# The output projection in a new order of tiles, with the operands of the MLP made beside it

## The chip, the cores and the metric

The kernel runs on one core of one Trainium2 chip. The metric is the device time of one execution in microseconds. A core has TensorE (PE in the rows; PEld is its weight load), VectorE (DVE), ScalarE (ACT), GpSimd (POOL) and SyncE (SP), which issues most of the DMAs; DMAs are also issued from ACT. Each engine, and each queue of DMA issues, works through its instructions in order.

## The reference

One pre-norm decoder layer on 2048 tokens of width 1024: a token mixer (gated DeltaNet heads and dilated sliding-window attention heads), then a gated MLP with a causal depthwise convolution, then a final RMSNorm. The part around the change:

```python
x = x + jnp.concatenate([y_a, y_b], axis=-1) @ w_out[l]        # output projection
h = rmsnorm(x, ln2[l])
gate = causal_dwconv(h @ w_gate[l], ffn_conv[l])
x = x + (jax.nn.silu(gate) * (h @ w_up[l])) @ w_down[l]
```

## The kernel before

Every product of float32 numbers is made of three products of split numbers: an operand is cast to a high part on ACT and the rest is taken as a low part on DVE (`split`, L67 and L68), and `mm3` (L73 to L75) multiplies high by high, high by low and low by high.

The tokens are 16 tiles of 128. The output projection (`Mlp.out_proj`, L1025) takes one tile at a time: it loads the mixer's results for these tokens (`yg`, L1046, and `ys`, L1049, both in runs of 512 bytes), splits them, runs 48 matmuls of 512 columns, loads the tile of `x` (L1069), adds (L1072), and stores the sum as `x1` (L1073). `norm2` (L952) then works on the tile before: square and sum on ACT, two small steps on GpSimd (L902, L903), scaling on DVE (L958, in place, so it waits until `x1` is stored), eight transposes on TensorE (L962) that stand behind the next tile's matmuls, two copies on ACT (L963) and a store to `hT` in memory (L965). The first three tiles run seven of their eight row blocks ahead (`HEAD`).

The MLP (`gate_up`, L1083) works in two halves of 1024 tokens. A half is a 2 x 2 arrangement of blocks: two blocks of 512 tokens (b = 0 is the half's first four tiles, b = 1 its second four) by two halves of the width (kh). It is multiplied by a scheme of seven products, so there are seven operands s = 0 to 6, each a high and a low tile `hc[s]`. Operands 0 and 3 are parts of block 0 alone, 1 and 4 are differences of both blocks, 2 and 6 are built on those. A pass p goes through the seven steps for two blocks of 128 hidden columns; there are eleven passes for each half. Each step has 24 matmuls and needs two weight operands, made two steps ahead (`prep`): for s = 1, 2, 4 and 5 from sums on GpSimd (L1119 to L1129). The results leave the banks `g` and `sc`, `pv`, `tp` by copies on ACT (L1204) or additions on DVE (L1202).

Operands of the first half are made by `form` (L967), 512 columns at a time, from `hT`. For the second half four operands (1, 2, 4, 6: `EARLY`) are made ahead by `foresee(j)` (L994), which takes tile j of both blocks: loads of 256 KB (L1002), one to three subtractions on GpSimd (L1010), the split on GpSimd too, and two stores of 256 KB to `hf` (L1015). `recall` loads them when the second half begins; the other three are made by `form(1, s)`. `foresee`'s results take their buffers from the same three as `xt` and, later, `cv`; the loads of `form` and `foresee` share four buffers `sm`.

The order before: tiles 0 to 7, then 8, 12, 9, 13, 10, 14, 11, 15. From the eleventh place on (i >= 10) three steps of `form(0, 0..3)` follow each tile, from the thirteenth two steps of `foresee`. Eight of its 16 steps are left for gate_up, one in each of the passes p = 1 to 8. The last tile's `norm2` (`late`) comes in gate_up's first steps, with both transposes in bank `pv`; `form(0, 4..6)` in its first three.

Of the kernel before, what the change touches and what calls it, by code (L numbers as in the profile page):

```python
# [9 lines left out]
F32 = mybir.dt.float32  # L10
F32R = mybir.dt.float32r
BF16 = mybir.dt.bfloat16
AF = mybir.ActivationFunctionType
ALU = mybir.AluOpType
# [917 lines left out]
class Mlp:  # L932
# [19 lines left out]
    def norm2(self, xt, t, tag=None):  # L952
# [6 lines left out]
        for j in range(2):  # L959
            tp = n.bank(4, tag)  # L960
            for k in range(4):
                nc.tensor.transpose(tp[:, k, :], xt[:, (4 * j + k) * P:(4 * j + k + 1) * P], n.ident)  # L962
            nc.scalar.copy(xt[:, 512 * j:512 * j + 512].rearrange("p (k t) -> p k t", k=4), tp)  # L963
# [30 lines left out]
    def foresee(self, j):  # L994
# [10 lines left out]
        for s, first, rest in ((1, (1, 0), ((0, 0),)), (4, (1, 1), ((1, 0),)), (2, (0, 0), ((1, 1), (1, 0))),  # L1005
# [10 lines left out]
            yield  # L1016

    def recall(self, s):
        n = self.n
# [5 lines left out]
    def out_proj(self):  # L1025
        n, a = self.n, self.n.a
        nc, tc, v = n.nc, n.tc, n.nc.vector
        with ExitStack() as eo:
# [28 lines left out]

            first = (x for s in range(4) for x in self.form(0, s))
            for t in range(HEAD):
                out_proj(t, range(7))  # L1060
            early = self.early = (x for j in range(4) for x in self.foresee(j))
            for i, t in enumerate((*range(8), 8, 12, 9, 13, 10, 14, 11, 15)):
                out_proj(t, range(7, 8) if t < HEAD else range(8))
                if t >= HEAD:
                    for j in list(xts)[:2]:
# [7 lines left out]
                nc.sync.dma_start(n.x1[t], xt)  # L1073
                if i >= 10:
                    for _ in range(3):
                        next(first, None)
                if i >= 12:
                    next(early)
                    next(early)
            assert next(first, 1)  # L1080
            self.late = lambda: [self.norm2(xts[j], j, "pv") for j in list(xts)]

    def gate_up(self):  # L1083
# [7 lines left out]
        spare = dict(zip(("sa", "sb", "r01"), three))  # L1091
        steps = [(half, p, s) for half in range(2) for p in range(NP) for s in range(7)]
        raws, sums, made = {}, {}, {}
# [85 lines left out]
        for i, (half, p, s) in enumerate(steps):  # L1179
# [17 lines left out]
            for m in range(2):  # L1197
# [5 lines left out]
                else:  # L1203
                    nc.scalar.copy(dst, ps)  # L1204
            if half == 0:
                if p == 0 and s < 3:
                    for _ in self.form(0, s + 4):
                        pass
                if p == NP - 1:
                    if s in EARLY:  # L1210
                        self.recall(s)
                    else:
                        for _ in self.form(1, s):
                            pass
                elif p and s == 4:
                    next(self.early, None)
            if i == 1:
                self.late()
            if s == 5:
# [235 lines left out]
```

## Time and profile before

| | us |
|---|---|
| runs shown | 2839.38, 2845.15, 2848.18 |
| their median | 2845.15 |
| the profiled execution | 2836.76 |
| its span, first to last instruction | 2835.0 |

The rows of the section below come from that one profiled execution; times in them count from the start of its span. A row of the timeline has the start, the duration, the engine, the line, the operation and, in brackets, how long the engine had been idle before it and what ended that. In a row of groups, the numbers behind the bar are busy time, mean nanoseconds of one, and idle time before them.

### The profile page before, as it was taken

The page shows a single profiled execution, that of the slowest core. Times are in us where ns is not written, and L with a number is a line of the kernel's source. Part 1 is how long each engine was busy: PE and PEld are TensorE (multiplying, and loading weights), DVE is VectorE, ACT ScalarE, POOL GpSimd, SP SyncE. Part 2 cuts the span into 40 slices and gives each one's busy share as a digit, 9 for nine tenths or more (in the row PEclk, how much of TensorE's full clock was granted, in tenths as well). Part 3 has the DMA queues.
Part 4 walks back from the last instruction along what each step waited for, and adds up shares of the span by engine and source line. Part 5 has one row for each costly group of instructions (what it writes and reads, how often), then busy time and mean ns, then how long its engine had stood idle before and what let it go on. Part 6 is the DMA issues. An engine that isn't in the chain of part 4 may idle for free. (4 is left out here: it accounts for less than half of the span.)

```text
span 2835.0 us, 41316 instructions
## 1 busy us (share of the span) xinstructions
PE 2716.6 (96%) x14974; PEld 2278.4 (80%) x14974; DVE 1682.6 (59%) x2758; ACT 1111.2 (39%) x2333; POOL 1149.3 (41%) x1363
## 2 busy tenths in 40 slices
PE   8999999899999999989968999999999998999999
PEld 8998777777798998877856777777888887788887
DVE  4205544823655655644337878878877787545464
ACT  5313545252056666563224333324333333322243
POOL 4300223132244444411165777766656664312231
PEclk9999999999899999999989999999999999999999
DMA  5222343377676656347684444446333333865553
GB/s 184 81 57 96 114 133 125 104 218 209 177 197 177 181 167 171 96 125 225 199 258 134 123 138 122 127 130 237 104 104 93 112 104 128 317 232 174 184 196 136
DMA packets 398490, 438.71 MB, mean 155 GB/s; under 512 B 84247, under 2 KB 289351, under 8 KB 396871
## 3 DMA queue, kind: packets, MB, share of 16 engines
q1 hardware_dynamic: 350672, 406.76, 46.2%
q10 hardware_dynamic: 45390, 20.90, 2.8%
q0 software_dynamic: 2224, 8.42, 1.0%
q8 instruction: 118, 1.93, 0.3%
q14 instruction: 86, 0.70, 0.1%
HBM read 295.79 MB, written 140.18 MB: 154 GB/s over the span
## 5 line engine op out<-in xcount | busy, mean ns | idle before, releaser
L68 DVE TENSOR_TENSOR wl<-wr,wh 128x512 fp32r<-128x512 f32 x220 | 304.7, 1417 | 69.8 <-ACT wh L67 68.7
L67 ACT CAST wh<-wr 128x512 fp32r<-128x512 f32 x220 | 136.2, 624 | 241.2 <-POOL wr L1119 119.8
L1165 POOL TENSOR_TENSOR sm<-cv 128x512 f32<-128x512 f32 x110 | 183.7, 1701 | 38.7 <-issue 26.7
L1249 POOL TENSOR_TENSOR w<-w,w 128x512 f32<-128x512 f32 x55 | 91.7, 1688 | 228.7 <-DMA w<-in_w_down_dram 223.3
L651 DVE CUSTOM_DVE_ANT_0 s<-sc,bias 128x256 f32<-128x256 f32 (+1 forms) x384 | 121.4, 362 | 104.8 <-PE sc L643 85.1
L67 ACT CAST ah<-ar 128x1408 fp32r<-128x1408 f32 x56 | 77.1, 1378 | 251.8 <-PE tp L74 70.1
L741 PE MATMUL pv<-pt,sv 128*65 128x128 f32 x1200 | 159.9, 276 | 6.3 <-ACT pt L723 5.9
L713 ACT ACTIVATE s<-s,nm 128x256 f32<-128x256 f32 (+1 forms) x384 | 151.8, 460 | 35.6 <-POOL rb L788 25.7
L73 PE MATMUL g<-hch,wh 128*128 128x512 f32 x352 | 143.2, 407 | 23.5 <-ACT g L1204 13.1
L75 PE MATMUL g<-hch,wl 128*128 128x512 f32 x352 | 142.5, 405 | 6.4 <-DVE wl L68 6.3
L741 PEld LDWEIGHTS pv<-pt,sv 128*65 128x65 f32 x1200 | 135.4, 139 | 11.0 <-ACT pt L723 10.2
L74 PE MATMUL g<-hcl,wh 128*128 128x512 f32 x352 | 142.0, 403 | 0.0
L73 PE MATMUL sc<-hch,wh 128*128 128x512 f32 x352 | 139.5, 396 | 1.8 <-ACT u L1204 1.1
L75 PE MATMUL sc<-hch,wl 128*128 128x512 f32 x352 | 139.1, 395 | 0.4 <-DVE wl L68 0.4
L74 PE MATMUL sc<-hcl,wh 128*128 128x512 f32 x352 | 139.2, 396 | 0.0
L74 PE MATMUL tp<-hcl,wh 128*128 128x512 f32 x352 | 139.0, 395 | 0.0
L73 PE MATMUL tp<-hch,wh 128*128 128x512 f32 x352 | 139.0, 395 | 0.0
L75 PE MATMUL tp<-hch,wl 128*128 128x512 f32 x352 | 139.0, 395 | 0.0
L723 ACT COPY pt<-tp 128x512 f32<-128x512 f32 (+1 forms) x152 | 87.3, 577 | 94.0 <-PE tp L720 57.3
L1145 DVE SCALAR_TENSOR_TENSOR cv<-g,fcw,cv 128x1024 f32<-128x1024 f32 x88 | 123.1, 1399 | 1.5
L580 POOL CAST qc<-q 128x256 fp32r<-128x256 f32 x128 | 79.9, 640 | 106.4 <-PE sc L643 102.8
L331 POOL TENSOR_SCALAR ss<-ss 128x8 f32<-128x8 f32 x16 | 3.3, 204 | 289.0 <-ACT junk L330 289.0
(379 smaller groups left out, 8284.9 us busy)
## 6 DMA issues: line engine op xcount, KB each, us to landing
ar<-act SPq DMA_DIRECT2D x56, 704.0 KB, 4.1
w<-in_w_down_dram SPq DMA_DIRECT2D x132, 256.0 KB, 5.1
act<-sm SPq DMA_DIRECT2D x110, 256.0 KB, 2.4
sm<-hT SPq DMA_DIRECT2D x92, 256.0 KB, 4.6
r<-in_w_gate_dram SPq DMA_DIRECT2D x66, 256.0 KB, 3.1
r<-in_w_up_dram SPq DMA_DIRECT2D x66, 256.0 KB, 4.2
xt<-in_x_dram SPq DMA_DIRECT2D x32, 512.0 KB, 4.5
zn<-zn SPq DMA_DIRECT2D x32, 512.0 KB, 5.4
```

The lines of the kernel that those rows point to most:

```text
L67: (first or nc.scalar.copy)(hi, src)
L68: (e or nc.vector).tensor_tensor(lo, src, hi.bitcast(F32), op=ALU.subtract)
L73: nc.tensor.matmul(ps, ah, bh, start=start, stop=False, skip_group_check=more)
L74: nc.tensor.matmul(ps, ah, bl, start=False, stop=False, skip_group_check=more)
L75: nc.tensor.matmul(ps, al, bh, start=False, stop=stop, skip_group_check=more)
L651: n.mark = v.tensor_tensor_reduce(out=s[:, r], in0=ps[:, r], in1=self.bias[d][:, bo:bo + r.stop - r.start], scale=1.0, scalar=-3e38, op0=A ...
L713: nc.scalar.activation(s, s, AF.Exp, bias=nm[:, col:col + 1])
L723: nc.scalar.copy(pts[g][:, 0:o], tp[:, 0:o])
L741: nc.tensor.matmul(dst, self.vcols(h, d, u, back), pt[:, j * P:(j + 1) * P], start=(back == int(prev)), stop=(back == 0))
L1145: v.scalar_tensor_tensor(cv, g[:, j:j + 1024], self.cw[:, x, j:j + 1], cv, op0=ALU.mult, op1=ALU.add)
L1165: gp.tensor_tensor(src, x(*op_[0]), x(*op_[2]), op=ALU.add if op_[1] > 0 else ALU.subtract)
L1249: gp.tensor_tensor(wsum[i, k], wsum[i, k], t, op=ALU.add if op[1] > 0 else ALU.subtract)
```

## The change

The projection takes the second half's tokens first, and in pairs: tile j of block 0, tile j of block 1. All 16 steps of `foresee` follow the tiles of places 4 to 11, two each. For the first half, operands 0 to 3 are made by a new function, `piece(j, s)`, 128 tokens at a time, from the fifth to last place on: two after each of the last four tiles, six after the loop, and the two that need the last tile, (3, 1) and (3, 2), after gate_up's first step, behind that tile's `norm2`, whose transposes now go to the banks `g` and `sc`. The first pass of gate_up takes its steps in the order 0, 3, 1, 2, 4, 5, 6.

```diff
-            tp = n.bank(4, tag)
+            tp = n.bank(4, tag and tag[j])
...
+    def piece(self, j, s):
+        n = self.n
+        nc, v, gp = n.nc, n.nc.vector, n.nc.gpsimd
+        c = slice(j * P, j * P + P)
+        k4 = lambda x: x.rearrange("p (k t) -> p k t", k=4)
+        if self.hc[s] is None:
+            self.hc[s] = tuple(self.hcp[s].tile([P, 4, 512], F32R, tag=f"h{i}{s}", name=f"hc{i}{s}") for i in "hl")
+        def load(b, kh):
+            r = self.small()
+            nc.sync.dma_start(k4(r), n.hT[b].rearrange("p (k t) -> p k t", k=KT)[:, 4 * kh:4 * kh + 4, c])
+            return r
+        if s in (0, 3):
+            r = load(0, s > 0)
+        elif s == 1:
+            r, o = load(1, 0), load(0, 0)
+            gp.tensor_tensor(r, r, o, op=ALU.subtract)
+        else:
+            r = load(1, 1)
+            h, l = (x[:, :, c].bitcast(F32) for x in self.hc[1])
+            gp.tensor_tensor(k4(r), k4(r), h, op=ALU.subtract)
+            v.tensor_tensor(k4(r), k4(r), l, op=ALU.subtract)
+        split(nc, self.hc[s][0][:, :, c], self.hc[s][1][:, :, c], k4(r))
...
-            first = (x for s in range(4) for x in self.form(0, s))
-            for t in range(HEAD):
+            early = (x for j in range(4) for x in self.foresee(j))
+            order = [x + y + z for x in (8, 0) for y in range(4) for z in (0, 4)]
+            pieces = [(j, s) for j in range(2) for s in range(4)] + [(2, 0), (3, 0), (2, 3), (3, 3), (2, 1), (2, 2)]
+            for t in order[:HEAD]:
                 out_proj(t, range(7))
-            early = self.early = (x for j in range(4) for x in self.foresee(j))
-            for i, t in enumerate((*range(8), 8, 12, 9, 13, 10, 14, 11, 15)):
-                out_proj(t, range(7, 8) if t < HEAD else range(8))
-                if t >= HEAD:
+            for i, t in enumerate(order):
+                out_proj(t, range(7, 8) if i < HEAD else range(8))
+                if i >= HEAD:
...
-                if i >= 10:
-                    for _ in range(3):
-                        next(first, None)
-                if i >= 12:
+                if 4 <= i < 12:
                     next(early)
                     next(early)
-            assert next(first, 1)
-            self.late = lambda: [self.norm2(xts[j], j, "pv") for j in list(xts)]
+                if i >= 12:
+                    for _ in range(2):
+                        self.piece(*pieces.pop(0))
+            last, = xts.items()
+            for x in pieces:
+                self.piece(*x)
+            self.late = lambda: (self.norm2(*last[::-1], ("g", "sc")), self.piece(3, 1), self.piece(3, 2))
...
-        steps = [(half, p, s) for half in range(2) for p in range(NP) for s in range(7)]
+        steps = [(half, p, s) for half in range(2) for p in range(NP)
+                 for s in (range(7) if half + p else (0, 3, 1, 2, 4, 5, 6))]
...
+            if i == 0:
+                self.late()
             if half == 0:
-                if p == 0 and s < 3:
-                    for _ in self.form(0, s + 4):
+                if p == 0 and i < 3:
+                    for _ in self.form(0, i + 4):
                         pass
...
-                elif p and s == 4:
-                    next(self.early, None)
-            if i == 1:
-                self.late()
```

## Rows read from the trace of the kernel before

**Rows 1.** The page, first part: busy time of each engine, share of the span, instructions.
```profile
PE 2716.6 (96%) x14974; PEld 2278.4 (80%) x14974; DVE 1682.6 (59%) x2758; ACT 1111.2 (39%) x2333; POOL 1149.3 (41%) x1363
```
**Rows 2.** Waits of TensorE, 1285 to 1500: total us, times, longest.
```profile
PE g L962 <- DVE xt L958: 13.2, 5, 5.3
```
**Rows 3.** Waits of TensorE, 1500 to 2380.
```profile
PE g L73 <- ACT g L1204: 13.1, 6, 4.8
```
**Rows 4.** Windows: length, busy us per engine, granted clock, DMA share, GB/s.
```profile
1366.00:1378.00 12.00, 12.00 (x57) 9.77 (x57) 3.82 (x5) 2.99 (x6) 0.74 (x2) 1.00 0.56 174
...
1426.00:1438.00 12.00, 9.95 (x35) 8.26 (x36) 9.95 (x9) 3.99 (x6) 9.14 (x7) 0.72 0.55 157
1438.00:1450.00 12.00, 10.62 (x50) 8.44 (x49) 3.27 (x4) 0.33 (x2) 7.08 (x8) 1.00 1.01 295
...
1474.00:1486.00 12.00, 1.97 (x8) 1.57 (x8) 3.17 (x4) 2.32 (x4) 8.23 (x10) 0.54 0.97 279
1486.00:1498.00 12.00, 7.37 (x17) 4.56 (x18) 4.01 (x5) 2.86 (x5) 5.66 (x7) 0.61 0.81 267
```
**Rows 5.** Timeline of SP: stores of `x1` of two clean tiles.
```profile
1352.62 0.32 SPq L1073 DMA_DIRECT2D x<-xt  x1
...
1364.69 0.32 SPq L1073 DMA_DIRECT2D x<-xt  x1
```
**Rows 6.** Timeline of TensorE: transposes behind the last projection tiles, and gate_up's start.
```profile
1428.05 0.47 PE L962 MATMUL g<-ident,xt 128*128 128x128 f32 x1 [3.75 <-DVE xt L958]
...
1444.44 0.66 PE L962 MATMUL g<-ident,xt 128*128 128x128 f32 x4 [1.38 <-DVE xt L958]
...
1457.98 0.66 PE L962 MATMUL g<-ident,xt 128*128 128x128 f32 x4 [1.23 <-DVE xt L958]
...
1475.61 1.11 PE L962 MATMUL g<-ident,xt 128*128 128x128 f32 x4 [5.32 <-DVE xt L958]
...
1487.76 0.80 PE L73 MATMUL g<-hch,wh 128*128 128x512 f32 x1 [10.19 <-ACT wh L67]
...
1517.37 0.80 PE L73 MATMUL pv<-hch,wh 128*128 128x512 f32 x1 [5.29 <-ACT xt L963]
```
**Rows 7.** Timeline of SP: the first weight load of gate_up.
```profile
1482.05 0.47 SPq L1103 DMA_DIRECT2D r<-in_w_gate_dram  x1
```
**Rows 8.** Timeline of TensorE: first matmul of p = 1, 10 (first half), 1, 10 (second).
```profile
1542.69 0.40 PE L73 MATMUL g<-hch,wh 128*128 128x512 f32 x1
...
1916.10 0.40 PE L73 MATMUL g<-hch,wh 128*128 128x512 f32 x1
...
2002.54 0.39 PE L73 MATMUL g<-hch,wh 128*128 128x512 f32 x1
...
2355.34 0.39 PE L73 MATMUL g<-hch,wh 128*128 128x512 f32 x1
```
**Rows 9.** Timeline of GpSimd in pass 3 of the first half.
```profile
1653.96 3.21 POOL L1010 TENSOR_TENSOR sm<-sm 128x512 f32<-128x512 f32 x2 [7.39 <-DMA sm<-hT]
...
1664.44 1.30 POOL L1119 TENSOR_TENSOR wr<-r,r 128x512 f32<-128x512 f32 x1 [2.87 <-DMA r<-in_w_gate_dram]
```
**Rows 10.** Groups of instructions, 1290 to 1500.
```profile
L958 DVE SCALAR_TENSOR_TENSOR xt<-xt,ss,lnb 128x1024 f32<-128x1024 f32 x16 | 21.5, 1347 | 41.5 <-POOL ss L903 22.8 <-DMA x<-xt 17.9 <-ACT xt L963 0.8
...
L67 ACT CAST hch<-sm 128x512 fp32r<-128x512 f32 x16 | 9.6, 621 | 51.1 <-POOL sm L983 18.1 <-DVE sm L988 17.8 <-DMA sm<-hT 15.2
```
**Rows 11.** Timeline of one clean tile: transposes, store of the rows.
```profile
1339.62 0.60 PE L962 MATMUL g<-ident,xt 128*128 128x128 f32 x4
...
1341.64 0.58 ACTq L965 DMA_DIRECT2D hT<-xt  x1
```
**Rows 12.** DMA issues, 1290 to 1500: count, KB each, median us to landing.
```profile
sm<-hT SPq DMA_DIRECT2D x46, 256.0 KB, 4.8
...
hT<-xt ACTq DMA_DIRECT2D x15, 512.0 KB, 4.6
```
**Rows 13.** Timeline of GpSimd: stores of the last heads' rows, four blocks.
```profile
1278.95 2.36 POOL L790 DMA_DIRECT2D ys<-rbl  x4 [1.88 <-DVE rbl L788]
```

## Prediction

> **What bounds the kernel now.** I read the page first: TensorE is busy for 96% of the span [rows 1], so only stretches where it waits or runs at the lower clock can give time back. Next the table of waits, in two stretches. In the output projection TensorE waits above all for the scaled rows that it is to transpose (`xt`, L958) [rows 2]; in gate_up it waits for ACT to empty the `g` bank, six times, 13.1 us [rows 3]. Then the windows, for what lies behind the first: a clean tile of the projection loads the DMA engines to 0.56, while from the place where `foresee` starts they reach 0.97 to 1.01, and the granted clock falls to 0.72, 0.54 and 0.61 in three of the windows [rows 4]. Last the timeline of TensorE, for what each stretch loses against an undisturbed one.
>
> A clean tile takes 12.07 us (1352.62 to 1364.69) [rows 5]. A projection tile's matmuls end where the gap before its transposes begins, start minus gap: 1424.30, 1443.06, 1456.75 and 1470.29 for the last four places [rows 6]. The last three tiles so take 18.76, 13.69 and 13.54 us, 45.99 where three clean ones take 36.21: **9.8 us lost**. From the last projection matmul to the first of gate_up (1487.76) pass **17.5 us**, with the gate weight's cast as the last thing waited for; its load was issued only at 1482.05 [rows 6, 7]. The first pass (p = 0, first half) takes 1542.69 - 1487.76 = 54.93 us [rows 6, 8]. A clean pass takes 39.20: nine of the second half, 2002.54 to 2355.34, take 352.80 [rows 8]. So the first pass loses **15.7 us**: halved clock, and 5.29 where bank `pv` still held the late transposes [rows 4, 6]. The nine passes p = 1 to 9 of the first half take 1916.10 - 1542.69 = 373.41, **20.6 us** more than the nine clean ones [rows 8]. What the first half has there and the second has not is `foresee`: GpSimd waits 7.39 us for its loads with the weight sums queued behind it, and these then wait another 2.87 for weights whose loads stand behind foresee's transfers on SP [rows 9]. Without the stall at the turn to the second half, which the change leaves alone, the losses in reach are 9.8 + 17.5 + 15.7 + 20.6 = 63.6 us.
>
> **The change, part by part.**
>
> *Eight foresee steps leave gate_up.* Passes 1 to 9 then look like the second half's: **-20.6**. Bounds: -20.6, and 0 if the stalls are not theirs. I take -20.6: the waits on `g` stand only where the steps stand [rows 3, 8, 9].
>
> *All 16 steps now lie under eight projection tiles, two each* (places 4 to 11; they run under the tile that follows). By the code they are 44 loads and 32 stores of 256 KB, 2.49 MB per tile. A clean tile moves 174 GB/s x 12 us = 2.09 MB [rows 4]. At 295 GB/s, which is what the DMA engines moved when fully busy [rows 4], 4.58 MB take 15.5 us, against 12.07 us of matmuls: the projection turns from TensorE-bound to DMA-bound, 3.45 us x 8 = 27.6 us. The first such tile starts with a gap of 3.75, as before [rows 6]. **+31.** Below: the last two tiles before, 13.6 us each under foresee and form at once (but without loads of `yg` and `ys`, all issued by then): 8 x 1.5 = +12. Above: the first of them, 18.8 us, eight times: +54; with a gap as before the last transposes (5.32), +62. I stay with the bytes, because the windows from 1438 and from 1474 show the engines full, not waiting [rows 4]. In that regime the half clock after a gap costs little: TensorE has 3.4 us per tile to spare. GpSimd holds each tile's two small scaling steps behind foresee's subtractions, which wait for loads; ACT's square, the scaling and the transposes queue behind that [rows 2, 10]. This is the path by which the DMA time reaches TensorE.
>
> The page "DMA: Bandwidth & Descriptors" of the Trainium skill (Where 436 GB/s comes from) puts the limit between HBM and SBUF near 358 GB/s. By it 4.58 MB would take 12.8 us and the eight tiles would lose 5.8 instead of 27.6; the trace's fully busy windows, 279 and 295 GB/s, do not agree.
>
> *The last four places carry pieces instead of form and foresee.* Ten loads in four tiles, 0.66 MB a tile on 2.09 MB, is 9.3 us at 295 GB/s, below 12.07; the `xt` buffers are no longer shared with foresee's results. **-9.8**; bounds -9.8 and 0. The casts and differences of the pieces are as many as form's, 0.62 us each on ACT [rows 10], under matmuls.
>
> *The turn to gate_up.* The first step needs piece (3, 0): tile 3 is transposed only after the last tile's matmuls, and its rows go out to memory and back. From transposes to issue of the store 2.0 us (1339.62 to 1341.64) [rows 11]; store 4.6, load 4.8 [rows 12]; cast 0.62 [rows 10], plus the difference: 12.5 us where 17.5 stand now: **-5.0**. On SP this load waits for the store, and behind it may stand the eight weight loads of the first pass, for which the first matmuls wait as well. If they come after it, the gap stays at 17.5; with faster landings it could be 10. I take 12.5: now the weight load stands behind foresee's work and late `x` loads, which are gone.
>
> *The first pass.* The last tile's transposes move from `pv` to `g` and `sc` and can run inside that gap: the 5.29 goes. The order 0, 3, 1, 2 starts with the two operands that need block 0 alone, so tile 7's way through memory (some 12 us) and the subtractions lie beside two steps, 11 us at full clock. The start at half clock stays, about 4 us (0.61 over 12 us) [rows 4]; 2 for late operands and weights. Loss 6 instead of 15.7: **-9.7**; bounds 3 and 15.7.
>
> *Tiles 8, 12 and 9 at the head.* They need the third and fourth block of the last heads' rows, four stores issued within 2.36 us [rows 13]. At worst 2.4 us later, under 42 matmuls for each of three tiles that need none of it; **0**. If that cover were gone it would cost those 2.4.
>
> **Sum.** 31 - 9.8 - 5.0 - 9.7 - 20.6 = -14.1 us. The profiled execution took 2836.76 us (span 2835.0 and 1.76 around it), so 2822.7; the median of the three runs is 8.4 above it, and on that I put **2831.0 us**, 0.5% faster. About 0.3%, 8.5 us, is what a measurement of this kernel can tell from no change.
>
> **Rivals.** The sum turns on one figure, the time of a tile under two foresee steps; the change breaks even at 12.07 + 45.1 / 8 = 17.7 us, and from 18.8 it is slower by 0.3%.
>
> *The clock falls at every tile* (ends slower). If each of the eight tiles goes as the first one did, 18.8 us with the clock at 0.72 [rows 4, 6], up to 20.8 with the 5.32 gap, mid 19.8, the loss is 62: -14.1 + 31 = +16.9, 2862. For it: each gap over 3.7 us before stands beside a window with a low clock [rows 4, 6]. Against: gaps of 1.38 and 1.23 left it at 1.00, and the next two tiles held 13.6. The Trainium skill's page "TensorE: Matmul & The Clock Gate" (Why this matters for your kernels) says that idle gaps between bursts of matmuls drop the array to its lower clock; the trace agrees.
>
> *The transfers hide better*, 13.6 us a tile as in the last two: loss 12, -33, 2812. Against: those two loaded no `yg` and `ys`.
>
> *The turn wins nothing*: the weight loads queue behind piece (3, 0) on SP, gap and first pass stay: -14.1 + 14.7 = +0.6, 2846.
>
> *The stalls of gate_up stay*, being GpSimd's own load and not foresee's: +6.5, 2852. The clean second half speaks against it [rows 8].
>
> **Chances and range.** The forecast's case (tiles of 14.1 to 16.9 us, so losses of 16 to 39, 2816 to 2839) 0.53; clock 0.17; better hiding 0.14; turn 0.11; gate_up 0.05. The forecast's case is faster by over 0.3% but for the slowest fifth (0.42 of 0.53), better hiding always: 0.56. Same: 0.11 of the forecast's, 0.09 of the turn, 0.02 of gate_up: 0.22. Slower: the clock, 0.02 of the turn and 0.03 of gate_up: 0.22. The range goes from better hiding, 2810, to the clock's, 2860; its own range is 2816 to 2839.
>
> **What would show it.** The eight tiles at places 5 to 12 come every 15 to 16 us with a DMA share near 1, then three at 12.1; gate_up's first matmul 12 to 13 us after the last projection matmul; first pass near 45; passes 1 to 9 in 353 with no wait on `g`. Wrong if the tiles come at 13 or 19 us, if weights are what the first step waits for, or if passes 1 to 9 still stall.

## The result, and the profile of the changed kernel

The changed kernel takes 2860.56 us (median of five runs, 2849.71 to 2871.32), the kernel before 2847.18 beside it (five runs, 2839.38 to 2850.64): ratio 1.0053, interval 1.0032 to 1.0073. It is 0.5% slower, where 0.5% faster was forecast, and lies just above the range. A second set of six runs (e9_again below) gave 1.0054, 1.0034 to 1.0075. The profiled execution took 2871.32 us, with a span of 2869.5.

The first part of the page, against [rows 1], shows the same matmuls with 22 us more of PE busy and a span 34.5 us longer, so the page alone does not say where the time went:

```profile
span 2869.5 us, 41313 instructions
## 1 busy us (share of the span) xinstructions
PE 2739.0 (95%) x14974; PEld 2301.8 (80%) x14974; DVE 1666.6 (58%) x2758; ACT 1113.7 (39%) x2333; POOL 1132.6 (39%) x1363
```

For that the span is cut at landmarks of TensorE's timeline: the projection's first transposes (L962), its last matmul, the first matmul of gate_up, the first matmul of each pass. In us:

| | mixer, to the first transposes | projection from there | turn | first pass | passes 1 to 9 | first pass of the second half | the rest |
|---|---|---|---|---|---|---|---|
| before | 1312.0 | 158.1 | 17.6 | 54.9 | 373.4 | 47.3 | 518.8 |
| after | 1332.9 | 186.7 | 14.7 | 64.0 | 352.8 | 46.6 | 519.1 |
| difference | +20.9 | +28.6 | -2.9 | +9.0 | -20.6 | -0.7 | +0.2 |

(Passes 1 to 9 of the second half, 352.8 in both, are left out, and pass 10 of the first half is in "the rest"; the differences are of the unrounded times.)

The mixer is not touched by the change, and its 20.9 us are not the change's: over the eighteen profiles of this study this part took between 1312 and 1334 us; in e9_again, the same changed kernel, 1320.6, and in e11_before_lean, a variant of the kernel before, 1328.8. Without it the changed part comes to **+13.6** (+15.2 in e9_again), and the medians differ by 13.4. So the parts are compared below, and not the spans of single executions. Each part is read from one profile. Where nothing in it was changed, the projection's stage took 184.1 to 187.4 us (five profiles) and the first pass 63.5 to 64.3 (six), so a difference of 1 or 2 us says little.

**The projection.** The windows of TensorE's time under foresee (columns as in [rows 4]):

```profile
1342.00:1354.00 12.00, 9.28 (x46) 7.59 (x45) 6.26 (x7) 4.89 (x9) 5.46 (x6) 0.94 0.98 304
...
1390.00:1402.00 12.00, 7.41 (x25) 6.23 (x26) 3.64 (x4) 2.22 (x4) 7.16 (x7) 0.57 0.95 280
...
1438.00:1450.00 12.00, 10.98 (x40) 9.10 (x41) 2.25 (x3) 2.32 (x4) 7.57 (x7) 0.72 0.91 274
...
1462.00:1474.00 12.00, 5.41 (x15) 3.90 (x16) 3.64 (x3) 2.54 (x4) 5.79 (x7) 0.50 0.87 258
...
1498.00:1510.00 12.00, 12.00 (x57) 9.81 (x56) 6.22 (x8) 4.83 (x9) 1.29 (x3) 1.00 0.50 164
...
1522.00:1534.00 12.00, 0.00 (x0) 0.00 (x0) 5.14 (x7) 3.92 (x9) 6.91 (x7) 0.55 0.92 276
```

In the eleven windows of this length from 1342 to 1474, four of which stand here, the DMA share is 0.86 to 1.02 at 249 to 304 GB/s, where a clean tile before had 0.56 [rows 4]. The clock fell to 0.57, 0.72 and 0.50 in three windows of this stage. From 1498 on, with the pieces alone beside it, a tile is clean again: TensorE busy throughout, share 0.50. In the window from 1522 TensorE has nothing at all; that is the turn. The table of waits, 1315 to 1530, has four waits for scaled rows where there were five of 13.2 us [rows 2]:

```profile
PE g L962 <- DVE xt L958: 28.0, 4, 13.2
```

TensorE's timeline (columns as in [rows 6]) has the three long ones between tiles that wait for nothing:

```profile
1363.34 0.60 PE L962 MATMUL g<-ident,xt 128*128 128x128 f32 x4
...
1375.43 0.60 PE L962 MATMUL g<-ident,xt 128*128 128x128 f32 x4
...
1394.59 1.12 PE L962 MATMUL g<-ident,xt 128*128 128x128 f32 x4 [6.91 <-DVE xt L958]
...
1409.37 0.60 PE L962 MATMUL g<-ident,xt 128*128 128x128 f32 x4
...
1421.45 0.66 PE L962 MATMUL g<-ident,xt 128*128 128x128 f32 x4
...
1439.02 1.11 PE L962 MATMUL g<-ident,xt 128*128 128x128 f32 x4 [5.26 <-DVE xt L958]
...
1467.96 1.12 PE L962 MATMUL g<-ident,xt 128*128 128x128 f32 x4 [13.16 <-DVE xt L958]
```

The long waits lie in or next to the windows with the low clock. The loss is not spread evenly: from 1363.34 to 1375.43 and from 1409.37 to 1421.45 a tile takes 12.1 us, as a clean one does, and the tile behind the wait of 6.91 takes 14.8 (1394.59 to 1409.37) in the window at 0.57. Of the 38.0 us that the stage loses (e8_all_left below), 28.0 are the four waits.

**The turn and the first pass.** The same timeline further on, with the first matmul of p = 1 last:

```profile
1520.04 0.60 PE L962 MATMUL sc<-ident,xt 128*128 128x128 f32 x4
1534.30 0.80 PE L73 MATMUL g<-hch,wh 128*128 128x512 f32 x1 [13.67 <-ACT hch L67]
...
1543.19 0.60 PE L962 MATMUL g<-ident,xt 128*128 128x128 f32 x4
...
1555.98 0.80 PE L73 MATMUL tp<-hch,wh 128*128 128x512 f32 x1 [6.16 <-ACT hch L67]
1572.28 0.51 PE L73 MATMUL g<-hch,wh 128*128 128x512 f32 x1 [2.52 <-ACT g L1234]
1590.69 0.77 PE L73 MATMUL g<-hch,wh 128*128 128x512 f32 x1 [6.96 <-DVE g L1232]
...
1598.27 0.40 PE L73 MATMUL g<-hch,wh 128*128 128x512 f32 x1
```

The gap of the turn, 13.67 us, lies empty: the last tile's transposes stand at 1543.19, behind all 24 matmuls of the first step. What ends the gap is the cast of the first step's operand, on ACT; its rows come from the transposes at 1520:

```profile
1521.34 0.52 ACTq L965 DMA_DIRECT2D hT<-xt  x1
...
1533.11 0.62 ACT L67 CAST wh<-wr 128x512 fp32r<-128x512 f32 x1 [3.70 <-POOL wr L1149]
1533.64 1.66 ACT L67 CAST hch<-sm 128x512 fp32r<-128x512 f32 x3
```
```profile
1528.34 2.02 SPq L1029 DMA_DIRECT2D sm<-hT  x4
```

The load is issued 7.0 us after the store, and loads of this kind landed 2.9 us after their issue here (median of six, 1515 to 1540), so near 1531.2. The cast comes some 2.4 us later: on ACT it stands behind that of a weight sum (`wh`), which waits for GpSimd.

What follows from the late transposes is on ACT's and SP's timelines, ACT's store of these rows first:

```profile
1545.72 0.52 ACTq L965 DMA_DIRECT2D hT<-xt  x1
```
```profile
1550.19 1.48 SPq L1029 DMA_DIRECT2D sm<-hT  x3
1551.76 23.17 SPq L977 DMA_DIRECT2D sm<-hT  x15
```

The rows go to memory at 1545.72, the late pieces load at 1550.19, and the operand that they complete is what the step at 1555.98 waited 6.16 us for. The loads for operands 4 to 6 (L977) stand behind the pieces on SP: the fifteen of this row start at 1551.76 and take 23 us to issue. The fifth and seventh step then wait 2.52 and 6.96 us, both for bank `g` to be emptied. The fifth waits for a copy on ACT that stands behind two casts of operand 4, which wait for their differences, as these do for their loads. The seventh waits for an addition on VectorE (L1232), which works without a pause from 1579.16 on; GpSimd's timeline beside it is the second block:

```profile
1579.16 0.68 DVE L68 TENSOR_TENSOR wl<-r,wh 128x512 fp32r<-128x512 f32 x1
...
1586.53 1.75 DVE L988 TENSOR_TENSOR sm<-sm,hcl 128x512 f32<-128x512 f32 x1
1588.20 1.75 DVE L68 TENSOR_TENSOR hcl<-sm,hch 128x512 fp32r<-128x512 f32 x1
1589.88 0.67 DVE L1232 TENSOR_TENSOR g<-g,g 128x512 f32<-128x512 f32 x1
```
```profile
1586.02 1.71 POOL L1149 TENSOR_TENSOR wr<-r,r 128x512 f32<-128x512 f32 x1
1587.80 1.60 POOL L1153 TENSOR_TENSOR wr<-wr,r 128x512 f32<-128x512 f32 x1
```

Operations of one size take 1.75 us on VectorE while GpSimd works beside them, and 0.67 or 0.68 where it rests as they start. All six between 1579.8 and 1589.9 are of the long kind, which the prediction did not reckon with. In all the first pass takes 24.8 us more than a clean one (39.20): 15.6 are the three waits, and most of the rest is the lower clock behind the waits (0.74 granted from 1534 to 1546; the first step takes 8.9 us, the seventh 7.6, a clean one 5.6).

**Passes 1 to 9.** Between 1598.27 and 1951.07 (the first matmul of p = 10) lie 352.80 us, nine times 39.20; the six waits for `g` [rows 3] are gone.

### The profile page after: what moved, and what is told of

It reads as the page before. It is cut to its first block, busy times and chain, and to the rows that moved or that the text cites. A ratio compares the mean times of both kernels' runs of the same rounds, so it can differ in the third digit from the quotient of the medians.

```text
span 2869.5 us, 41313 instructions
## 1 busy us (share of the span) xinstructions
PE 2739.0 (95%) x14974; PEld 2301.8 (80%) x14974; DVE 1666.6 (58%) x2758; ACT 1113.7 (39%) x2333; POOL 1132.6 (39%) x1363
## 4 chain that ended last, share of the span: by engine, by line
PE 80%; DMA 8%; POOL 4%; DVE 3%; ACT 2%; issue 2%; SPq 1%; ACTq 0%; POOLq 0%; DVEq 0%
PE tp L75 6%; PE tp L74 6%; PE tp L73 6%; PE sc L74 6%; PE sc L75 6%; PE sc L73 6%; PE pv L75 5%; PE pv L74 5%; PE pv L73 5%; PE g L75 4%; PE g L74 4%; PE g L73 4%; PE pv L741 3%; DMA sm<-hT 2%; PE sc L642 2%
## 5 line engine op out<-in xcount | busy, mean ns | idle before, releaser
L68 DVE TENSOR_TENSOR wl<-wr,wh 128x512 fp32r<-128x512 f32 x220 | 264.9, 1233 | 50.4 <-ACT wh L67 49.2
L741 PEld LDWEIGHTS pv<-pt,sv 128*65 128x65 f32 x1200 | 139.7, 143 | 12.1 <-ACT pt L723 11.1
L67 ACT CAST wh<-r 128x512 fp32r<-128x512 f32 x88 | 50.7, 620 | 169.1 <-PE sc L74 89.1
```

What stands on the lines that cost most here:

```text
L67: (first or nc.scalar.copy)(hi, src)
L68: (e or nc.vector).tensor_tensor(lo, src, hi.bitcast(F32), op=ALU.subtract)
L741: nc.tensor.matmul(dst, self.vcols(h, d, u, back), pt[:, j * P:(j + 1) * P], start=(back == int(prev)), stop=(back == 0))
```

## The experiments

Ratios are to the kernel before on the same chip, with a 95% interval; where none stands, it is a single run. Stage, turn and first pass are the columns of the table above, each read from that run's profile. Line numbers of the variants are shifted by a few lines against the changed kernel.

### What foresee costs beside the projection

**e8_all_left**: the floor of the projection. No foresee beside it; its 16 steps lie in gate_up, two in each of the passes 1 to 8.

```diff
-                if 4 <= i < 12:
-                    next(early)
-                    next(early)
...
+            if half == 0 and 0 < p < NP - 1 and s in (1, 4):
+                next(self.early, None)
```

> The changed kernel with all 16 steps of foresee left in gate_up, two in each of the passes 1 to 8, none beside the projection. Theory (a step costs 2.9 us beside the projection and 2.1 in gate_up, as two runs showed): the projection falls to 147 to 152 us, TensorE's own time; passes 1 to 9 rise to 385 to 395. Rival (gate_up has no room for two steps a pass): 410 us or more.

A single run, 2890.12 us. Stage 148.75, as expected: against this the changed kernel loses 38.0 us in the projection and the kernel before lost 9.4, where the prediction read 9.8. Passes 1 to 9 take 414.82, which is the rival's case (410 or more) and not the 385 to 395 expected: two steps in a pass cost 62.0 over nine clean passes, 3.9 each. The waits for `g` of [rows 3] are back, and more (waits, 1500 to 2420):

```profile
PE g L73 <- ACT g L1231: 31.4, 9, 4.9
```

**e4_half_left**: the changed kernel with eight of the 16 steps left in gate_up, one in each pass.

```diff
+            if half == 0 and 0 < p < NP - 1 and s == 4:
+                next(self.early, None)
```
(and one `next(early)` fewer beside each tile)

> The changed kernel, with one step of foresee instead of two behind each of the eight tiles, and the other eight steps left in gate_up's passes 1 to 8, as in the kernel before. Theory (bytes, and the stalls of the passes belong to foresee): 3.34 MB a tile, 12.0 us at 278 GB/s, so the projection is bound by TensorE again: 186.7 us become 152 to 160; passes 1 to 9 go back from 352.8 to about 373; the whole falls by about 8 to 14 us, ratio to the kernel before 1.000 to 1.003. Rival (the passes' stalls came from elsewhere): passes 1 to 9 stay at 353 and the ratio falls to 0.994.

2857.4 us over ten runs, 1.0029 (1.0016 to 1.0042). Stage 163.82, passes 369.52. By its bytes the stage should have come to 152 to 160, with TensorE alone as the limit; that was missed, so something besides the bytes holds it. Eight steps cost 15.1 us in the projection (163.82 - 148.75), the next eight 22.9, 2.86 each; in gate_up eight cost 16.7, 2.09 each (in the kernel before 20.6, 2.58). So the half that the change moved costs more where it went than where it was.

**e3_off_gpsimd**: foresee's subtractions on VectorE, its split on ScalarE and VectorE.

```diff
-                gp.tensor_tensor(r, r, load(*x), op=ALU.add if add else ALU.subtract)
+                v.tensor_tensor(r, r, load(*x), op=ALU.add if add else ALU.subtract)
-            split(nc, t[:, 0], t[:, 1], r, gp, gp.tensor_copy)
+            split(nc, t[:, 0], t[:, 1], r)
```

> The changed kernel, with foresee's subtractions and lower parts on VectorE and its casts on ScalarE, none on GpSimd; the same loads and stores. Theory (bytes): the projection stays at 180 to 190 us from the first transposes to the last matmul, since the same 4.58 MB a tile go through. Rival (GpSimd's small scaling steps stand behind foresee's subtractions): they no longer do, and the stretch falls to 165 us or less.

A single run, 2843.56 us; stage 170.53, between the two theories: 16.2 of the 38.0 us went with GpSimd's part in foresee and 21.8 stay. Whether the 16.2 were GpSimd's order or its pace, this run does not tell apart. The same stretch of both kernels, first the changed one, then this:

```profile
1337.00:1481.00 144.00, 115.32 (x490) 92.39 (x489) 37.31 (x37) 29.03 (x47) 80.55 (x79) 0.87 0.95 280
```
```profile
1337.00:1481.00 144.00, 127.54 (x559) 102.06 (x558) 72.45 (x93) 45.86 (x76) 15.44 (x26) 0.95 1.01 300
```

The DMA engines are now full and move 300 GB/s. What is left is near what the bytes alone would cost: 4.58 MB at 300 GB/s are 15.3 us a tile, 25.6 us over eight clean ones (but see e6 below). The way from GpSimd to TensorE has two arms, to be seen in the groups of instructions of the changed kernel, 1330 to 1525 (behind the second bar: idle time before, and what ended it):

```profile
L958 DVE SCALAR_TENSOR_TENSOR xt<-xt,ss,lnb 128x1024 f32<-128x1024 f32 x14 | 21.4, 1530 | 51.7 <-DMA x<-xt 27.8 <-POOL ss L903 23.9
...
L1099 DVE TENSOR_TENSOR xt<-xt,pv 128x512 f32<-128x512 f32 x12 | 8.2, 686 | 44.2 <-DMA xt<-in_x_dram 43.5 <-PE pv L75 0.7
```

and of e3:

```profile
L958 DVE SCALAR_TENSOR_TENSOR xt<-xt,ss,lnb 128x1024 f32<-128x1024 f32 x13 | 16.7, 1283 | 14.2 <-DMA x<-xt 14.2
...
L1099 DVE TENSOR_TENSOR xt<-xt,pv 128x512 f32<-128x512 f32 x12 | 8.2, 687 | 24.2 <-DMA xt<-in_x_dram 19.8 <-issue 3.0 <-PE pv L75 1.3
```

One arm is the one that the prediction named, the two small steps in GpSimd's queue (23.9 us of idle time before the scaling, none in e3; the scaling itself fell from 1.53 to 1.28 us). The other is longer and was not named: the addition of `x` waits 43.5 us for the load of `x`, which stands on SP behind foresee's stores, and these wait for GpSimd's split. It also takes its buffer from the same three as foresee's results; which of the two holds it longer is not told apart here. SP's timeline of the changed kernel shows the order, stores of foresee (L1015), loads of foresee (L1002), then the store of `x1` and the load of `x` (L1096):

```profile
1384.56 1.74 SPq L1015 DMA_DIRECT2D hf<-hf  x2
1386.35 1.10 SPq L1002 DMA_DIRECT2D sm<-hT  x2
1387.56 0.44 SPq L1100 DMA_DIRECT2D x<-xt  x1
1388.10 0.38 SPq L1096 DMA_DIRECT2D xt<-in_x_dram  x1
```

**e2_lean**: each of the four blocks of a pair of tiles is loaded once, not up to three times, and results are built on one another: 16 loads instead of 44, 16 subtractions instead of 28.

```diff
+        x10, x00 = load(1, 0), load(0, 0)
...
+            if s == 1:
+                gp.tensor_tensor(x00, x10, x00, op=ALU.subtract)
...
+            elif s == 4:
+                x11 = load(1, 1)
+                gp.tensor_tensor(x10, x11, x10, op=ALU.subtract)
...
+            elif s == 2:
+                gp.tensor_tensor(x11, x11, x00, op=ALU.subtract)
...
+            else:
+                x01 = load(0, 1)
+                gp.tensor_tensor(x01, x01, x11, op=ALU.subtract)
```

> The changed kernel, with foresee loading each of its four blocks once for each tile pair (16 loads of 256 KB instead of 44, 16 subtractions on GpSimd instead of 28); stores as before. Theory (bytes: the projection is bound by the DMA engines at about 278 GB/s under foresee): 3.66 MB a tile instead of 4.58, 13.2 us instead of 17.3; from the first transposes to the last projection matmul 186.7 us become 155 to 162. Rival (the three shared buffers of xt and foresee's results bind): still 17 us a tile, 180 us or more. Second rival (GpSimd's order binds): three sevenths of the subtractions gone, 170 to 178 us.

2835.24 us, 0.9959 (0.9934 to 0.9983). Stage 163.47, just above the 155 to 162 expected: 23.3 of the 38.0 us are gone. With this edit alone the new order is faster than the kernel before.

**e7_lean_same_gp**: e2 with twelve subtractions added whose results nothing uses, so that GpSimd has 28 again.

> The changed kernel with the lean loads of foresee, but with as many subtractions on GpSimd as before: 12 of the 28 give values that are overwritten and never used. Theory (the lean version won by its bytes): the projection takes 163 to 169 us. Rival (it won by GpSimd's shorter queue): 176 us or more.

A single run, 2844.66 us; stage 169.36. Of the 23.3 us of e2, 17.4 are won by the 28 loads that are gone and 5.9 by the subtractions. The loads count with their bytes and with what waits for them on GpSimd and SP; these are not separated.

**e11_before_lean**: the kernel before with e2's foresee and nothing else.

> The kernel before, with the lean foresee (one load for each block) and nothing else of the change. Theory (half of foresee's cost is its bytes, in either place): the last tiles of the projection lose 4 to 6 us less and the passes with a step 4 to 9 us less; ratio 0.994 to 0.998. Rival (the old order hides the loads anyway): 0.999 or more.

2826.75 us, 0.9923 (0.9901 to 0.9945), more than was expected, but not where: the projection's stage, which was to fall by 4 to 6 us, went from 158.11 to 160.15, while passes 1 to 9 fall from 373.41 to 358.67 and the first pass from 54.93 to 47.08. The lean step wins in either order; it is no merit of the new one. With the lean step the new order, as the change has it, is not faster than this (0.9943 in e5 below).

### The turn and the first pass

**e1_early_norm**: the last tile's `norm2` is called right behind the loop, ahead of the first step's matmuls.

```diff
-            self.late = lambda: (self.norm2(*last[::-1], ("g", "sc")), self.piece(3, 1), self.piece(3, 2))
+            self.norm2(*last[::-1], ("g", "sc"))
+            self.late = lambda: (self.piece(3, 1), self.piece(3, 2))
```

> The changed kernel, with the last tile's norm2 right behind the projection instead of behind gate_up's first step; nothing else. Theory (the first pass of gate_up loses its 24.8 us because that tile's rows reach memory only after the first step, and the loads of the fifth to seventh operand stand behind theirs on SP): the transposes run inside the 13.7 us gap before gate_up, the first pass falls from 64.0 to about 46 us, the whole by 18 us against the changed kernel: ratio to the kernel before 0.998 to 1.000 instead of 1.005. Rival (the first pass is bound by its loads and the weight sums whatever the last tile does): the waits only move, first pass 58 us or more, ratio 1.003 or more.

2850.37 us over ten runs, 0.9997 (0.9982 to 1.0012). Turn and first pass fall from 78.67 to 69.31, 9.4 where 18 were expected: the wait for the late piece is gone, but the first pass, at 57.17, is nearer to the rival's 58 than to the 46 expected, since the fifth step now waits 6.5 us and the seventh 4.0 (waits of TensorE, 1480 to 1600; of the two in the first row the longer is the turn's):

```profile
PE g L73 <- ACT hch L67: 8.6, 2, 4.7
PE g L73 <- ACT g L1235: 6.5, 1, 6.5
```

The ratio fell by 0.0056, some 16 us; the stages show 9.4 of them, and the two intervals leave room for that.

**e10_other_rows**: e1 with operands 4 to 6 of the first half made from the second half's rows, which are in memory long before; this part of the computation is changed.

```diff
-            nc.sync.dma_start(r, n.hT[2 * half + b][:, c:c + 512])
+            nc.sync.dma_start(r, n.hT[2 + b if s >= 4 else 2 * half + b][:, c:c + 512])
```

> The early norm2 alone, and operands 4 to 6 of the first half made from the second half's rows, which are in memory long before, instead of the first half's (so this part of the computation is another one; loads, subtractions and splits are as many). Theory (what is left of the first pass's loss comes from these operands: each of their loads takes 512 tokens, the last tile among them, so all 16 wait for it): the first pass falls from 57.2 to 44 to 49 us. Rival (the four load buffers or the sums of the weights bind): 54 us or more.

A single run, 2860.2 us; first pass 57.39, as in e1 (57.17). The theory fell: the last tile's rows are not what operands 4 to 6 wait for once `norm2` is early.

**e13_borrowed** and **e15_three_sm**: e1 with more load buffers, and with fewer. In e13 the second load of each of operand 4's differences goes into a buffer of `xt`, free at that time (`other` is true for these loads alone); e15 has three buffers `sm` instead of four.

```diff
-            r = self.small()
+            r = self.wk.tile([P, D], F32, tag="xt", name="xo", bufs=3)[:, :512] if other else self.small()
```

> The changed kernel with the last tile's norm2 right behind the projection loop (as e1_early_norm), and in the first half's operand 4 the second load of each difference goes into one of the three buffers of xt, which are free there, so that the first pass's loads have seven buffers instead of four. e1 took 57.17 us for the first pass, e10_other_rows 57.39 with operands 4 to 6 made from other rows, so the last tile's way through memory doesn't hold them. Theory (the four load buffers hold the loads of operands 4 to 6 back, behind the late pieces and the weight sums on GpSimd): first pass at most 51 us, with the wait on operand 4's cast (6.5 us in e1) below 2. Rival (the order of work on GpSimd, DVE and ACT holds them, or the transfers themselves): at least 55 us. Everything else as in e1.

> The same kernel as e1_early_norm with three load buffers instead of four, the opposite direction. Theory (load buffers bind): first pass at least 62 us instead of 57.2, and the projection's stage, where foresee takes two to four of these buffers for one step, longer as well: 195 us or more instead of 187. Rival (engine order or transfers bind): first pass 56 to 59, stage 185 to 190.

A single run each. e13, 2846.24 us: first pass 51.80 against 57.17, 5.4 less, though not quite the 51 expected; the wait at the fifth step is still 5.4, where below 2 was expected, and at the seventh there is none. e15, 2851.76 us: first pass 56.72 and stage 188.60, both as with four buffers; the turn grew, from 12.14 to 15.73, and the second half's first pass fell from 46.29 to 42.22, which is not explained. So a place of their own for half of operand 4's loads won 5.4 us, but three buffers did the first pass and the projection no harm: that a shortage of buffers is the reason is not shown.

**e16_copies_on_dve**: e14_half_borrowed (below), with the third and fourth step's results copied out of the banks by VectorE.

> The kernel of e14_half_borrowed, but in the first pass the third and fourth step's results are copied out of their banks by VectorE instead of ScalarE. In e13 and e14 what is left of the first pass's loss is one wait of 5.4 and 5.1 us at its fifth step: for ScalarE's copy of bank g, which stood behind four casts of operand 5 that were waiting for their loads. Theory (the place in ScalarE's queue is the wait): the first pass falls from 52.67 to at most 49 us, with no wait over 2.5 us at the fifth step; ratio 0.987 to 0.990. Rival (VectorE's queue holds the low parts of the same casts, so the copies wait there as long): first pass 51.5 us or more, ratio as e14 (0.989).

2817.57 us, 0.9889 (0.9867 to 0.9912), the ratio of e14; but the first pass rose from 52.67 to 57.74, the rival's case, and the waits went with the copies to the other engine (waits, 1480 to 1600):

```profile
PE g L73 <- DVE g L1246: 6.1, 1, 6.1
...
PE sc L73 <- DVE u L1246: 4.5, 1, 4.5
```

The copy of `g` waits on either engine behind the splits of operands that wait for their loads. What remains of the first pass's loss is thus not the choice of the engine; whether an order with the copies ahead of these splits would win it was not tried.

### Better versions, and the repeat

| | edit | us | ratio | stage | first pass | passes 1 to 9 |
|---|---|---|---|---|---|---|
| e9_again | the changed kernel once more | 2861.34 | 1.0054 (1.0034 to 1.0075) | 186.24 | 64.25 | 352.80 |
| e5_lean_early | e2 and e1 | 2830.63 | 0.9943 (0.9924 to 0.9962) | 163.76 | 57.71 | 352.80 |
| e6_lean_off_early | e5 and e3 | 2825.34 | 0.9920 (0.9898 to 0.9942) | 159.08 | 56.30 | 352.80 |
| e12_lean_half | e5 and e4 | 2825.05 | 0.9917 (0.9897 to 0.9937) | 152.95 | 57.58 | 355.52 |
| e14_half_borrowed | e12 and e13 | 2812.89 | 0.9891 (0.9865 to 0.9917) | 151.20 | 52.67 | 354.86 |

> The changed kernel itself, once more. Theory (the change costs some 13.6 us in the part that it touches; the profiled execution took 20.9 us more before that part begins, in a stretch with the same order of instructions, and that belongs to the execution and not to the change): ratio 1.003 to 1.007; the first transposes of the projection come anywhere from 1312 to 1333 us, and from there to the end the time is 1523 + 13 to 15 us. Rival (the change slows the mixer's phase too): the first transposes come at 1330 us or later again.

> The two edits of the first runs together: norm2 of the last tile right behind the projection, and foresee with one load for each block. Theory (the two losses are separate): from the first transposes to the last projection matmul 163 us as with the lean foresee alone, first pass and the gap ahead of it 62 us as with the early norm2 alone; 17 us below the lean foresee alone, ratio to the kernel before 0.988 to 0.992. Rival (what is won at the turn is lost again, because more loads then meet there): ratio 0.994 or more.

> As the last, and foresee's subtractions and splits on VectorE and ScalarE instead of GpSimd. Theory (with 3.66 MB a tile at the 303 GB/s that the DMA engines moved once GpSimd was out of the way, a tile takes 12.1 us, TensorE's own time): the projection falls from 163 to 150 to 156 us, ratio 0.984 to 0.989. Rival (with fewer bytes GpSimd no longer stands in the way): the projection stays at 160 us or more.

> The lean foresee and the early norm2 in the new order, with one step of foresee behind each of eight tiles and eight steps left in gate_up's passes. Theory (a lean step costs about 1.9 us beside the projection, (163.5 - 148.75) / 8 for two, and no less in gate_up): the projection falls from 164 to 151 to 156 us and the passes rise from 352.8 to 360 to 370; no gain against all 16 beside the projection, ratio 0.993 to 0.997. Rival (a lean step is hidden in gate_up): passes at 356 or less, ratio 0.990 or less.

> The version of e12_lean_half (each block of foresee loaded once, norm2 of the last tile behind the loop, eight steps of foresee left in gate_up) with the borrowed buffers for operand 4. e12: ratio 0.9917, first pass 57.58. Theory (buffers bind): first pass at most 51, so 6 us or more less: ratio 0.988 to 0.991. Rival: first pass at least 55, ratio 0.9905 to 0.993.

e5 keeps the stage of e2 and the first pass of e1, as expected, but stands 8.7 us under e2 in turn and first pass together, not 17, and its ratio is in the rival's range (0.994 or more). e6 was to bring the stage to 150 to 156 and came to 159.08: at 3.66 MB a tile and 300 GB/s a tile would take 12.2 us, nearly TensorE's own time, and yet 10.3 us over the floor are lost. So bytes at the measured rate are not the whole of what is left once GpSimd is out of the way; what else holds it is open. In e12 the passes came out as the rival had it (356 or less). In e14 the first pass missed the 51 expected, and the ratio came out as forecast.

e12 tells how a lean step is best placed: eight of them cost 4.2 us in the projection (152.95 - 148.75) and the other eight 2.7 in gate_up (355.52 - 352.80), where eight old steps cost 15.1 and 16.7. Half and half, as the kernel before had it, beats all in the projection (e5) by 8 us of these two parts, though the intervals of the two ratios overlap. e14, and e16 with it, is the fastest point found, 1.1% under the kernel before; its interval overlaps those of e6, e11 and e12.

## Why the prediction was wrong, point by point

| term | predicted | measured |
|---|---|---|
| foresee beside the projection | +31 | +38.0 |
| last four places | -9.8 | -9.4 |
| turn | -5.0 | -2.9 |
| first pass | -9.7 | **+9.0** |
| passes 1 to 9 | -20.6 | -20.6 |
| the rest | 0 | -0.5 |
| sum | -14.1 | +13.6 |

The first two rows are told apart by e8's stage.

**The first pass is the step that failed.** It was predicted at 45 us and took 64; this term alone is off by 18.7 of the 27.7 us. The sentence was that the last tile's transposes "can run inside that gap" between the last projection matmul and the first of gate_up. But `late` is called behind step 0's matmuls (`if i == 0` stands after them in the diff), and TensorE works in order: the transposes came at 1543.19, nine microseconds after the gap's end. The prediction then let the way through memory "lie beside two steps, 11 us". Counted from the transposes to the first matmul that needs it, it took 12.8 us (1543.19 to 1555.98), about as estimated; but only one step, the second, lay beside it. e1 shows this cause by moving this one call: the wait of 6.16 us is gone, and 9.4 us come back, 6.8 of them in the first pass itself (63.97 to 57.17). The rest of the miss lies in the operands behind: the prediction put late operands and weights at 2 us, and the fifth and seventh step alone waited 9.5, where the loads of operands 4 to 6 come behind the late pieces on SP and what empties the banks stands behind their splits. e13 wins 5.4 us of this by loading half of operand 4 elsewhere; e10 shows that the last tile's rows are not the reason; e15 that three load buffers do as well as four; e16 that moving the copies to another engine does not help. VectorE's long operations beside GpSimd's are read from the rows above; no run moved either. What would bring the first pass from 52 to the predicted 45 stays open.

**foresee beside the projection was mis-sized**, 38.0 instead of 31. In the mean a tile took 16.8 us (12.07 + 38.0 / 8) where 15.5 and the start's gap had been set. It was under the break-even of 17.7, so this term alone would not have turned the sign. The mechanism was right in part: the DMA engines were busy for 0.95 of the stretch, and taking loads away won most (e2, e7). But the tiles did not come every 15 to 16 us, as transfers alone would have them; some came clean and some behind long waits. And in e4 the bytes fit under the matmuls, 12.0 us a tile by its expectation, and 15.1 us were still lost. The rate was too good for the kernel as it is: 280 GB/s at a share of 0.95, and 300 only when GpSimd's work was out of the way (e3), which is the prediction's 295. GpSimd's part in foresee held 16.2 us by e3, and 28 loads fewer at the same number of subtractions (e7) won 17.4; the two shares are not independent. The kernel before had a sign of it: while its first tile under foresee lost 6.7 us, the DMA share was 0.55 and GpSimd was busy for 9.14 of 12 us (the window from 1426 in [rows 4]), which transfers at their limit do not explain.

**The turn** was 14.7 instead of 12.5: the chain from transposes through memory to the cast was the right one, as the first step waits for `hch`. But from the store's issue to the load's it took 7.0 us where 4.6 had been set, the load 2.9 where 4.8, and the cast then stood some 2.4 us behind a weight's, for which nothing had been set.

**The last four places and passes 1 to 9** came out as predicted, and with them the reading that the stalls of gate_up were foresee's own.

**The rivals.** "The clock falls at every tile" gave 2862, close to what was measured, but not for its reason: three windows of this stage show a clock below 0.8, not eight, and the tiles took 16.8 us in the mean and not 19.8. (Its price was uneven, too: the first tile's 18.76 us with a gap of 5.32 for 3.75 are 20.3, a loss of 66 in eight, where 62 and, for the tile, 20.8 stand.) "The turn wins nothing" was nearest in kind, since it is the turn's and the first pass's order that decided, but it put the queueing on the weight loads; TensorE waited there for operands, and weights had their part only in the cast's 2.4 us. The clock's fall behind each long gap agrees with the Trainium skill ("TensorE: Matmul & The Clock Gate", Why this matters for your kernels), by which idle gaps between bursts of matmuls lower the clock: 0.57, 0.72 and 0.50 in the windows around gaps of 6.91, 5.26 and 13.16 us. The rate that the Trainium skill gives on the page "DMA: Bandwidth & Descriptors" (Where 436 GB/s comes from), some 358 GB/s, was not reached: 304 at most in the windows above, at a share of 0.98, and 300 over e3's 144 us, at 1.01.

## What to carry to other kernels

Work that is moved from a stage where it stalls a little to one where there "is room" has a price there, which is its bytes at that stage's measured rate plus the queues that it lengthens, and the second can be the larger part (e4); here eight steps cost 2.1 to 2.6 us each where they stood and 2.9 where they went. Cutting what the step moves (16 loads for 44) won more than any place for it, and won in the old order too. And before counting on a gap, find the moved instructions in the program order of the engine that has the gap: a call that stands behind a step's matmuls does not run ahead of them.

## What the hardware showed unexpectedly

The mixer, with the same work in both kernels, took 1312 us in the profiled execution of the kernel before and 1333 in that of the changed one. The windows of this part:

```profile
0.00:1312.00 1312.00, 1263.19 (x8726) 1107.18 (x8727) 658.34 (x1799) 602.88 (x1530) 393.08 (x821) 0.98 0.50 146
```
```profile
0.00:1332.00 1332.00, 1281.70 (x8723) 1124.65 (x8724) 658.93 (x1799) 601.82 (x1529) 391.89 (x821) 0.97 0.49 144
```

VectorE, ScalarE and GpSimd are busy for the same time within 1.2 us; TensorE is busy 18.5 us longer with the same number of matmuls, at a lower mean granted clock. By the clock records of the two traces TensorE was held at the lower of its two levels (half the rate of the other) for 51.2 us of this part in the one and 88.7 in the other; half of the 37.5 us between them is 18.8. So the span varies by some 20 us with how long TensorE is held there, in a part that the change does not touch, and what starts this was not found. It is more than this change's whole effect, and the reason to compare by stages or by medians.
